# Layer A's first output rows prepared by GpSimd alone, and layer B's weight loads issued ahead of its residual rows

## The chip, the cores and the metric

The kernel runs on one core of one Trainium2 chip. The time is that of one execution in device microseconds (us). Three runs of the kernel before gave 2417.16, 2417.48 and 2418.24 us; their median is 2417.48. In this text the engines have the names that the profile gives them: PE is TensorE (matrix products), DVE is VectorE, ACT is ScalarE, POOL is GpSimd, and SP is SyncE, which here only issues transfers. Each engine works through its own list of instructions in order and waits on semaphores for the others.

## The reference

Two layers of a decoder trunk over one sequence of 2048 tokens of width 1024, in float32. Layer A is causal attention with 16 heads of 64 and a forget bias; layer B is attention in a window of 128 keys with 4 key heads. What matters here is how each layer ends, with a gate, an output product and the residual:

```python
# layer A
o = fox_attention(q, k, v, log_f).reshape(b, s, WIDTH_A)
h = h + (o * jax.nn.silu(gate)) @ w_out_a[i]
# layer B
o = swa_sink_attention(q, k_shared, v_shared, sinks[j]).reshape(b, s, WIDTH_B)
h = h + (o * jax.nn.silu(gate)) @ w_out_b[j]
```

## The kernel before

A float32 product is made of three faster ones: each operand is split into a rounded high part and the low remainder (h and l in the names), and high by high, high by low and low by high are summed in PSUM. So one product of 128x128 by 128x512 over all 1024 input columns is 24 matmuls.

The program runs five stages one after the other: projections of layer A (until 592 us), attention of layer A (592 to 1434), the output product of layer A (1445 to 1622), projections of layer B (1622 to 2047), and attention of layer B with its output product (2047 to 2417).

**Attention of layer A** goes head by head. A head's 2048 queries are four chunks of 512, and a chunk `ch` needs 2·ch+2 steps of two key blocks, so there are 20 steps a head and 320 in all, numbered n from 0. Head 15, the last, has n = 300 to 319, and its last chunk n = 312 to 319. A step makes scores on PE (L1021, L1022 and masks), their exponential on ACT (L1028, L1037), a rounded copy on ACT (L1040), the low part on POOL (L1041, `pl = pf - ph`), a running sum on DVE (L1050), and three steps later (`V_LAG`) the product with the values on PE (L1065). Between the steps PE is fed matmuls of the gate (L1111), whose weights come by the loads of L1087 into the buffers `wr` and `st`, and whose results DVE and ACT finish (L1123 to L1125). The last two gate groups of 24 matmuls are kept back until the attention is through: one goes to the bank `mx`, the next to the bank `pb`. Behind them the output product begins.

**The rows of the output product** are made in pairs of heads, 128 rows by a chunk of 512 queries. For a pair, four inputs are loaded by SP: two halves of the attention's result (`om`, L1236, and `oc`, L1237), the gate (`gt`, L1238) and the reciprocals of the softmax sums (`rd`, two loads, L1241). `gated` then does five operations on 128x512: the sum of the halves (L1255), times the reciprocals (L1258), times the gate (L1261), the rounded copy on ACT (L1262), the low remainder (L1263). The product of one pair is 24 matmuls (L1303), and there are 32 pairs. The first two pairs are prepared while the attention still runs: pair 0 at step 309, pair 1 at step 316, with their loads issued at 299 and 311, all of their arithmetic on DVE but for the copy. From pair 2 on, the sum is POOL's. The loads of pairs 0, 1 and 2 use the same buffers `qn`, `wh`, `wl`, so a load waits until the pair before it has done with its buffer. The weights of the output product are split by ACT (L142) and DVE (L143) in the same stretch.

SP issues everything in the order in which the program's scheduler has put it: attention results and gate rows to be stored, the inputs of the pairs, and the kept gate groups' weights. A transfer that has to wait for a semaphore holds all those behind it.

**Attention of layer B** has steps of about 5.06 us: scores (L1386), transposes (L362), values (L1471), and twelve matmuls of the output product (L1532) between them. Two groups of 24 make a tile of 128 tokens. Each group gathers in the one bank `pb`; DVE adds the residual rows `xr` (L1538, buffer `sq`) and SP stores the sum (L1539). The rows `xr` are loaded by L1527, the weights of the product by eight loads of 1 MB (L1510, `wo`), which are issued at steps 4 to 8.

## Time and profile before

| | |
|---|---|
| median of three runs | 2417.48 us |
| profiled execution | 2418.75 us |
| its span, first to last instruction | 2417.0 us |
| PE busy in the span | 2402.1 us (99%) |
| DVE, ACT, POOL busy | 1746.5, 1261.1, 986.7 us |
| granted PE clock, mean | 0.998 |

The profiled execution is 1.27 us above the median, and 1.75 us of it lie outside the span. In rows of the timeline the first number is the start in us from the span's start, the second the duration in us, and the bracket at the end is how long the engine sat idle before it and for whom. In rows of a table by stretches the five numbers behind the first are the busy times of PE, PE's weight loads, DVE, ACT and POOL, then come the granted PE clock (1.00 is full speed), the share of the transfer engines that was busy, and GB/s. The instructions of SP are marked SPq.

### The profile page before, as it was taken

The page shows a single profiled execution, that of the slowest core. Times are in us where ns is not written, and L with a number is a line of the kernel's source. Part 1 is how long each engine was busy: PE and PEld are TensorE (multiplying, and loading weights), DVE is VectorE, ACT ScalarE, POOL GpSimd, SP SyncE. Part 2 cuts the span into 40 slices and gives each one's busy share as a digit, 9 for nine tenths or more (in the row PEclk, how much of TensorE's full clock was granted, in tenths as well). Part 3 has the DMA queues.
Part 4 walks back from the last instruction along what each step waited for, and adds up shares of the span by engine and source line. Part 5 has one row for each costly group of instructions (what it writes and reads, how often), then busy time and mean ns, then how long its engine had stood idle before and what let it go on. Part 6 is the DMA issues. An engine that isn't in the chain of part 4 may idle for free. (4 is left out here: it accounts for less than half of the span.)

```text
span 2417.0 us, 36270 instructions
## 1 busy us (share of the span) xinstructions
PE 2402.1 (99%) x11960; PEld 2028.6 (84%) x11960; DVE 1746.5 (72%) x4094; ACT 1261.1 (52%) x2504; POOL 986.7 (41%) x634
## 2 busy tenths in 40 slices
PE   9999999999999999999999999999999999999999
PEld 7888899988888888888888878888888888888887
DVE  7656667735998998988898976457766643677776
ACT  5433324322878788777878751135423321466664
POOL 0000000011887777777877752210011000388885
PEclk9999999999999999999999999999999999999999
DMA  6656555677654745575466459975434474765552
GB/s 192 203 168 190 154 152 171 194 229 231 192 153 136 223 128 171 149 232 153 124 206 156 145 165 298 300 260 153 131 97 128 149 264 143 241 214 181 183 183 75
DMA packets 357004, 436.03 MB, mean 180 GB/s; under 512 B 65296, under 2 KB 248624, under 8 KB 350640
## 3 DMA queue, kind: packets, MB, share of 16 engines
q1 hardware_dynamic: 348464, 403.30, 55.3%
q10 hardware_dynamic: 8352, 30.41, 4.4%
q8 instruction: 95, 1.56, 0.3%
q14 instruction: 93, 0.76, 0.1%
HBM read 273.69 MB, written 159.79 MB: 179 GB/s over the span
## 5 line engine op out<-in xcount | busy, mean ns | idle before, releaser
L798 PE MATMUL b<-wh,big 128*128 128x512 f32 (+3 forms) x2560 | 772.2, 374 | 1.4 <-ACT wh L509 1.3
L1041 POOL TENSOR_TENSOR big<-st,big 128x1024 fp32r<-128x1024 f32 (+1 forms) x320 | 659.1, 2080 | 248.5 <-ACT big L1040 170.5
L798 PEld LDWEIGHTS b<-wh,big 128*128 128x128 f32 x2560 | 470.6, 188 | 72.8 <-ACT wh L509 3.2
L798 PE MATMUL b<-wl,big 128*128 128x512 f32 (+3 forms) x1280 | 473.7, 370 | 0.8 <-DVE wl L510 0.8
L1050 DVE TENSOR_TENSOR ac<-ac,st 128x512 f32<-128x512 f32 (+3 forms) x576 | 353.1, 613 | 28.2 <-ACT ac L1044 13.1
L1037 ACT ACTIVATE st<-sc 128x512 f32<-128x512 f32 (+1 forms) x512 | 275.1, 583 | 107.8 <-PE sc L1031 45.8
L1065 PE MATMUL pa<-big 128*128 128x512 f32 (+3 forms) x1280 | 319.9, 366 | 0.7 <-POOL big L1041 0.6
L1040 ACT CAST big<-st 128x1024 fp32r<-128x1024 f32 (+1 forms) x320 | 294.7, 923 | 8.0
L798 PEld LDWEIGHTS b<-wl,big 128*128 128x128 f32 x1280 | 241.2, 189 | 36.7 <-DVE wl L510 4.5
L1065 PEld LDWEIGHTS pa<-big 128*128 128x128 f32 x1280 | 229.9, 190 | 37.4 <-POOL big L1041 1.9
L1021 PE MATMUL sc<-big 128*128 128x512 f32 (+3 forms) x640 | 234.2, 370 | 5.3 <-ACT st L1037 3.5
L518 ACT ACTIVATE sq<-b,r 128x512 f32<-128x512 f32 (+2 forms) x128 | 77.8, 608 | 302.2 <-PE b L798 302.2
L989 DVE TENSOR_REDUCE mt<-mx 128x1 f32<-128x384 f32 (+1 forms) x360 | 214.2, 598 | 27.1 <-PE mx L976 25.0
L1022 PE MATMUL sc<-big 67*128 67x512 f32 (+3 forms) x640 | 229.4, 367 | 0.0
L976 PE MATMUL mx<-big 66*128 66x512 f32 (+2 forms) x600 | 225.3, 379 | 0.0
L520 DVE TENSOR_REDUCE sm<-sq 128x8 f32<-128x512 f32 (+2 forms) x128 | 74.8, 585 | 140.0 <-ACT sq L518 139.9
L1111 PE MATMUL pb<-wh,wr 128*128 128x512 f32 x488 | 172.0, 395 | 0.0
L900 POOL MEMSET rot<- 128x512 bf16 x1 | 0.5, 525 | 419.0 <-PE pb L362 419.0
L1434 POOL TENSOR_TENSOR big<-big,tri 128x1024 fp32r<-128x1024 f32 x60 | 144.4, 2406 | 60.6 <-DVE big L1431 60.6
L984 DVE CUSTOM_DVE_ANT_0 mx<-mx,rot 128x384 f32<-128x384 f32 (+2 forms) x240 | 147.6, 620 | 28.0 <-PE mx L976 25.3
L1021 PEld LDWEIGHTS sc<-big 128*128 128x128 f32 x640 | 121.7, 190 | 29.2 <-ACT st L1037 5.8
L1022 PEld LDWEIGHTS sc<-big 67*128 67x128 f32 x640 | 122.2, 191 | 18.7
(285 smaller groups left out, 4125.9 us busy)
## 6 DMA issues: line engine op xcount, KB each, us to landing
wr<-wg ACTq DMA_DIRECT2D x58, 512.0 KB
va<-st SPq DMA_DIRECT2D x32, 512.0 KB
ka<-st SPq DMA_DIRECT2D x64, 256.0 KB
ut<-big SPq DMA_DIRECT2D x16, 1024.0 KB
big<-ka SPq DMA_DIRECT2D x16, 1024.0 KB
big<-qa SPq DMA_DIRECT2D x16, 1024.0 KB
qb<-st SPq DMA_DIRECT2D x64, 256.0 KB
big<-qb SPq DMA_DIRECT2D x16, 1024.0 KB
```

Of the source, the lines that this page charges most:

```text
L798: nc.tensor.matmul(ps[:, :n], u[tb // 4][:, dt, us], W[k][dt], start=(dt == 0 and i == 0), stop=(dt == NDT - 1 and i == 2),)
L976: mm = nc.tensor.matmul(ps, qb[:66, i * P : (i + 1) * P], kb[:66, k0:k1], start=True, stop=True,)
L984: nc.vector.tensor_tensor_reduce(out=ps, in0=ps, in1=mask_m[:, 512 - w :], scale=1.0, scalar=NEG, op0=ALU.add, op1=ALU.max, accum_out=f_(o),)
L989: nc.vector.reduce_max(o, ps, axis=AX.X)
L1021: nc.tensor.matmul(o, ka[:, ks], qa[:, qs], start=not (last and n_), stop=False)
L1022: nc.tensor.matmul(o, kb[:, ks], qb[:, qs], start=False, stop=not diag)
L1037: nc.scalar.activation(pf[:, off : off + w], ps[:, :w], AF.Exp, scale=HD**-0.5)
L1040: nc.scalar.copy(ph[:, :tw], pf[:, :tw])
L1041: nc.gpsimd.tensor_tensor(pl[:, :tw], pf[:, :tw], f_(ph[:, :tw]), ALU.subtract)
L1050: nc.vector.tensor_tensor(a_, a_, pf[:, off : off + w], ALU.add)
L1065: product = nc.tensor.matmul(pv[:, q0 : q0 + w], v[:, k, :], src[:, off : off + w], start=(p == 0 and n_ == 0 and i == 0), stop=(last and ...
L1111: nc.tensor.matmul(ps, w[:, dt // 2 % 2, wk, dt % 2, :], us[dt][uk], start=(dt == 0 and i == 0), stop=(dt == NDT - 1 and i == 2),)
```

## The change

In layer A, the five operations of pair 0 are all put on POOL, one behind each of the steps 288, 290, 292, 294 and 296, with its loads issued from step 284 on. The five operations of pair 1 are also all on POOL, behind its last low part (the operation of L1041) of step 319; its loads are issued from step 300 on. The rounded copy that ACT made is now POOL's third operation, which writes the product in the rounded type. In layer B, the weight loads of a step are issued before the step's matmuls of the output product and not at its end, and the first tile's residual rows are loaded in the middle of each of its two groups and not ahead of it. The loads of the later tiles' rows stay where they were but for the order against the PSUM allocation.

```diff
--- before.py
+++ after.py
@@ -43,8 +43,8 @@
 SUM_LAG = 5
 LOAD_AT = 7
 
-PREP_LOAD_AT = (299, 311)
-PREP_AT = (309, 316)
+PREP_LOAD_AT = (284, 300)
+PREP_AT = (288, 290, 292, 294, 296)
 
 RAW_AT = 302
 
@@ -119,11 +119,17 @@
         self.t.gated_load(s // NDT, s % NDT, self.tiles[s])
         self.loaded = s + 1
 
-    def prepare(self, s, engine=None, pin=False, first=None):
+    def prepare(self, s, engine=None, pin=False):
         if s % 4 == 0:
             self.Y[s // 4] = self.t.sb("big", [P, 4, 2, CH], F32R)
-        self.t.gated(self.y(s), self.tiles.pop(s), engine or self.t.nc.vector, pin, first)
+        self.t.gated(self.y(s), self.tiles.pop(s), engine or self.t.nc.vector, pin)
         self.ready = s + 1
+
+    def prepare_parts(self, s):
+        if s % 4 == 0:
+            self.Y[s // 4] = self.t.sb("big", [P, 4, 2, CH], F32R)
+        self.ready = s + 1
+        return self.t.gated_parts(self.y(s), self.tiles.pop(s))
 
     def y(self, s):
         return self.Y[s // 4][:, s % 4]
@@ -1210,10 +1216,14 @@
                 raw = self.sb("big", [P, NDT // 2, D])
                 for p in range(NDT // 2):
                     op.weight_load(p, raw[:, p])
-            if n in PREP_AT:
-                op.prepare(PREP_AT.index(n), nc.vector, True, nc.vector)
             if n in PREP_LOAD_AT:
                 op.load(PREP_LOAD_AT.index(n), ("qn", "wh", "qn", "wl"))
+            if n in PREP_AT:
+                if n == PREP_AT[0]:
+                    parts = op.prepare_parts(0)
+                next(parts)
+        for _ in op.prepare_parts(1):
+            pass
         op.load(2, ("qn", "wh", "qn", "wl"))
         for item, more in zip(pending, HELD):
             feed(fed + more)
@@ -1243,7 +1253,16 @@
                 in_=d["rd"][h : h + 1, cols].to_broadcast([HD, CH]),
             )
 
-    def gated(self, y, tiles, engine, pin=False, first=None):
+    def gated_parts(self, y, tiles):
+        m, c, g, rb = tiles
+        yh, yl = (y[:, k] for k in range(2))
+        for out, a, b, op in (
+            (m, m, c, ALU.add), (m, m, rb, ALU.mult), (yh, m, g, ALU.mult),
+            (m, m, g, ALU.mult), (yl, m, f_(yh), ALU.subtract),
+        ):
+            yield self.tc.keep_in_program_order(self.nc.gpsimd.tensor_tensor(out, a, b, op))
+
+    def gated(self, y, tiles, engine, pin=False):
 
 
 
@@ -1252,9 +1271,7 @@
         nc = self.nc
         m, c, g, rb = tiles
         yh, yl = (y[:, k] for k in range(2))
-        add = (first or nc.gpsimd).tensor_tensor(m, m, c, ALU.add)
-        if pin and first is not None:
-            self.tc.keep_in_program_order(add)
+        nc.gpsimd.tensor_tensor(m, m, c, ALU.add)
         mult = engine.tensor_tensor(m, m, rb, ALU.mult)
         if pin:
             self.tc.keep_in_program_order(mult)
@@ -1523,11 +1540,11 @@
                 rows = slice(i * P, (i + 1) * P)
                 for nh in range(2) if i else (1, 0):
                     ns = slice(nh * CH, (nh + 1) * CH)
-                    xr = self.sb("sq", [P, CH])
-                    nc.sync.dma_start(out=xr, in_=res[rows, ns])
-
                     ps = self.ps("fl" if (i, nh) == (NTB - 1, 0) else "pb", [P, CH])
                     for p in range(NDT):
+                        if p == (0 if i else NDT // 2):
+                            xr = self.sb("sq", [P, CH])
+                            nc.sync.dma_start(out=xr, in_=res[rows, ns])
                         for n_, (y, k) in enumerate(((0, 0), (0, 1), (1, 0))):
                             nc.tensor.matmul(
                                 ps, yt(i, y, slice(p, p + 1))[:, 0, :],
@@ -1557,6 +1574,8 @@
                 php = self.sb("big", [P, 2, 2, 2, G, P], F32R)
             if n == V_LAG_B + NKV:
                 odd += [[self.sb(t, [P, 4, P], F32R) for _ in range(2)] for t in ("wh", "wl")]
+            for j in B_WEIGHTS_AT.get(n, ()):
+                weight_load(j)
             o = (n - O_LAG_B) * per
             feed(o + FEED_1)
             if n % NKV == 1 and NKV < n < N:
@@ -1575,8 +1594,6 @@
                     load(i + 1)
                 if g == NKV - 1 and i + 1 < NTB:
                     load_v(i + 1)
-            for j in B_WEIGHTS_AT.get(n, ()):
-                weight_load(j)
             yield
         feed(total)
```

The lines of the kernel move by 6 at the start and by 17 at the end: L1041 becomes L1047, L1087 L1093, L1236 to L1238 and L1241 become L1246 to L1248 and L1251, L1255 becomes L1274, L1532 L1549, L1527 L1547, L1510 L1527; the new function's operations are L1263.

The order in which the engines get their instructions changes in three places that matter below.

At the end of layer A's attention, on POOL. `big<-st,big` are the low parts of the last chunk's steps, `qn<-qn,wh` and its like the operations on a pair (x29 are the sums of the pairs from 3 on). Before:

```order
L1041 TENSOR_TENSOR big<-st,big 128x1024 x6
L1255 TENSOR_TENSOR qn<-qn,wh 128x512
L1041 TENSOR_TENSOR big<-st,big 128x896
L1041 TENSOR_TENSOR big<-st,big 128x384
L1255 TENSOR_TENSOR wh<-wh,wl 128x512 x29
```

and now:

```order
L1047 TENSOR_TENSOR big<-st,big 128x1024 x6
L1047 TENSOR_TENSOR big<-st,big 128x896
L1047 TENSOR_TENSOR big<-st,big 128x384
L1263 TENSOR_TENSOR qn<-qn,wh 128x512
L1263 TENSOR_TENSOR qn<-qn,wl 128x512
L1263 TENSOR_TENSOR big<-qn 128x512
L1263 TENSOR_TENSOR qn<-qn 128x512
L1263 TENSOR_TENSOR big<-qn,big 128x512
L1274 TENSOR_TENSOR qn<-qn,wh 128x512
```

Pair 1's five operations stand behind the last low part, and the sum of pair 2 (L1255, now L1274) behind them. DVE loses the eight operations of pairs 0 and 1, ACT two copies.

In the same place, on SP. `st<-wg` and `wr<-wg` are the weights of the two gate groups kept back, `wh<-oc`, `wl<-rd`, `qn<-om` and `qn<-gt` the inputs of pair 2. Before:

```order
L1237 DMA wh<-oc 128x512
L1241 DMA wl<-rd 64x512
L1236 DMA qn<-om 128x512
L1241 DMA wl<-rd 64x512
L1238 DMA qn<-gt 128x512
L1087 DMA st<-wg 128x1024
L1087 DMA wr<-wg 128x1024
L1087 DMA st<-wg 128x1024
L1236 DMA wh<-om 128x512
L1087 DMA wr<-wg 128x1024
```

and now:

```order
L1093 DMA wr<-wg 128x1024
L1093 DMA st<-wg 128x1024
L1247 DMA wh<-oc 128x512
L1251 DMA wl<-rd 64x512
L1246 DMA qn<-om 128x512
L1248 DMA qn<-gt 128x512
L1251 DMA wl<-rd 64x512
L1083 DMA om<-sq 64x512
L1132 DMA gt<-sq 128x512
L1084 DMA oc<-sq 64x512
L1093 DMA st<-wg 128x1024
L1093 DMA wr<-wg 128x1024
```

The first two weight loads serve the group in `mx`, the last two the group in `pb`. The inputs of pair 2 stood ahead of all four and waited for DVE's operations on pair 1; now they stand between the two groups' loads and wait for POOL's. `qn<-om` waits for pair 1's fourth operation and `qn<-gt` for its fifth.

In layer B, on PE, around the first tile's second group. `b` are scores, `fl` transposes, `pa` values, `pb` the output product. Before, from the end of the first group on:

```order
L1386 MATMUL b_21178<-big 128x256 x8
L362 MATMUL fl<-ident,st 128x128 x4
L1532 MATMUL pb<-big 128x512 x6
L1471 MATMUL pa<-big,qn 128x512 x2
L1471 MATMUL pa<-big,wh 128x512 x2
L1532 MATMUL pb<-big 128x512 x6
L1386 MATMUL b_21239<-big 128x256 x8
L362 MATMUL fl<-ident,st 128x128 x4
L1532 MATMUL pb<-big 128x512 x6
L1471 MATMUL pa<-big,qn 128x512 x2
L1471 MATMUL pa<-big,wh 128x512 x2
L1532 MATMUL pb<-big 128x512 x6
```

and now:

```order
L1403 MATMUL b_21178<-big 128x256 x8
L368 MATMUL fl<-ident,st 128x128 x4
L1488 MATMUL pa<-big,qn 128x512 x2
L1488 MATMUL pa<-big,wh 128x512 x2
L1403 MATMUL b_21237<-big 128x256 x8
L368 MATMUL fl<-ident,st 128x128 x4
L1488 MATMUL pa<-big,qn 128x512 x2
L1488 MATMUL pa<-big,wh 128x512 x2
L1403 MATMUL b_21296<-big 128x256
L368 MATMUL fl<-ident,st 128x128 x4
L1549 MATMUL pb<-big 128x512 x24
L1403 MATMUL b_21296<-big 128x256 x7
```

The second group's 24 matmuls were spread over two steps in four sixes; now they are one block that comes two steps later. On SP the four last weight loads stood behind the first residual rows and now stand ahead of them. On DVE the sum of the first group moves behind a whole further step.

## The prediction, made before the changed kernel was run

> **What bounds the kernel now.** The stages were read first: the table of stretches, then PE's waits.

> ```profile
> 592.00:1434.00 842.00, 835.97 (x4090) 693.57 (x4089) 750.34 (x1613) 669.49 (x1060) 660.32 (x321) 1.00 0.58 167
> 2047.00:2417.00 370.00, 366.16 (x1977) 315.22 (x1975) 266.41 (x626) 202.07 (x728) 247.91 (x168) 1.00 0.57 181
> 2400.00:2417.00 17.00, 13.16 (x59) 10.55 (x57) 3.82 (x8) 0.96 (x2) 0.00 (x0) 0.97 0.17 63
> PE sc L1021 <- ACT st L1037: 3.5, 2, 2.6
> PE sc L1021 <- ACT st L1028: 1.7, 1, 1.7
> ```

> PE is the bound in both stages that the change touches. Attention A leaves PE 6.0 us idle; two waits for the exponentials make 5.2 of them. Layer B's 3.84 us of idle time all lie in its last 17 us, behind the last product. So B has nothing to give where the change works; A can give those waits and what follows from them. The timeline shows where they lie:

> ```profile
> 1405.38 0.50 PE L1021 MATMUL sc<-big 128*128 128x512 f32 x1 [1.68 <-ACT st L1028]
> 1411.41 0.50 PE L1021 MATMUL sc<-big 128*128 128x512 f32 x1 [0.87 <-ACT st L1037]
> 1423.52 0.58 PE L1021 MATMUL sc<-big 128*128 128x256 f32 x1 [2.64 <-ACT st L1037]
> 1433.73 0.45 PE L1065 MATMUL pa<-big 128*128 128x256 f32 x2 [0.18 <-POOL big L1041]
> 1434.02 0.45 PE L1111 MATMUL mx<-wh,st 128*128 128x512 f32 x1
> 1439.82 0.50 PE L1111 MATMUL pb<-wh,st 128*128 128x512 f32 x1
> ...
> 1404.31 0.62 ACT L1262 CAST big<-qn 128x512 fp32r<-128x512 f32 x1 [4.54 <-DVE qn L1261]
> 1422.35 0.62 ACT L1262 CAST big<-qn 128x512 fp32r<-128x512 f32 x1 [4.56 <-DVE qn L1261]
> ```

> Twice ACT stands 4.5 us before a pair's rounded copy, because DVE is late with the product by the gate; the exponentials are queued behind that copy, and PE waits for them. DVE is late because POOL works beside it:

> ```profile
> 1399.45 2.29 DVE L1258 TENSOR_TENSOR qn<-qn,wl 128x512 f32<-128x512 f32 x1
> 1418.83 2.76 DVE L1258 TENSOR_TENSOR qn<-qn,wl 128x512 f32<-128x512 f32 x1
> 1421.62 0.69 DVE L1261 TENSOR_TENSOR qn<-qn 128x512 f32<-128x512 f32 x1
> 1413.40 7.64 POOL L1041 TENSOR_TENSOR big<-st,big 128x1024 fp32r<-128x1024 f32 x3 [0.51 <-ACT big L1040]
> ```

> An operation of this kind takes 0.69 us where POOL is idle (1421.62) and 2.3 to 2.8 beside POOL's low parts. The last PE wait has a second price, the granted clock (the number behind the five busy times):

> ```profile
> 1423.00:1424.00 1.00, 0.48 (x2) 0.49 (x3) 1.00 (x2) 1.00 (x3) 0.00 (x0) 0.50 0.54 164
> 1428.00:1429.00 1.00, 1.00 (x4) 0.72 (x3) 1.00 (x1) 1.00 (x2) 1.00 (x2) 0.50 0.31 107
> 1429.00:1430.00 1.00, 1.00 (x5) 0.82 (x4) 1.00 (x2) 1.00 (x2) 1.00 (x1) 0.67 1.20 188
> ```

> From 1423.5 until about 1429.3 PE ran at half rate, and 5.8 us of such work lose 2.9. Behind the gaps of 1.68 and 0.87 the clock stayed at 1.00.

> **The change, part by part: what layer A gains.** With the ten operations of pairs 0 and 1 off DVE and ACT, the copies that held the exponentials are gone. Gain: 1.68 + 0.87 + 2.64 + 0.18 + 2.9 = 8.3 us. PE would then come to the `mx` group at 1434.0 - 8.3 = 1425.7, and POOL's last low part, for which the last values product waited 0.18 us, ends at about T = 1425.4.

> **What pair 0 costs.** POOL gets five operations in steps 288 to 296. One takes 1.30 us, by the sum that POOL makes for pair 2:

> ```profile
> 1427.36 1.30 POOL L1255 TENSOR_TENSOR qn<-qn,wh 128x512 f32<-128x512 f32 x1
> 1362.00:1374.00 12.00, 12.00 (x60) 9.91 (x59) 10.88 (x24) 8.75 (x15) 10.18 (x5) 1.00 0.06 14
> ```

> In the 12 us at the end of head 14, POOL is busy 10.18, so 1.8 are free per 12, and a step has 2.4. An operation of 1.30 every two steps (4.8 us, 0.7 free) makes POOL late by about 0.6 each, 3 us over the five. Values are used three steps behind, which covers most of it: I take 0.5 us, between 0 (cover holds) and 3 (none does).

> **What pair 1 costs.** Its five operations begin at T and take 5 x 1.30 = 6.5 us, so the remainder is done at 1431.9 if nothing disturbs it. DVE's weight splits (L143) run in the same stretch, and these two engines disturb each other:

> ```profile
> 1427.88 6.88 DVE L143 TENSOR_TENSOR big<-big 128x1024 fp32r<-128x1024 f32 x3 [0.38 <-PE pb L1111]
> 1428.60 5.08 POOL L1041 TENSOR_TENSOR big<-st,big 128x896 fp32r<-128x896 f32 x2
> 1375.51 3.10 POOL L1041 TENSOR_TENSOR big<-st,big 128x896 fp32r<-128x896 f32 x2 [1.90 <-PE sc L1027]
> 1435.29 1.21 DVE L143 TENSOR_TENSOR big<-big 128x1024 fp32r<-128x1024 f32 x1
> ```

> The same two low parts took 5.08 us beside three splits and 3.10 elsewhere. So POOL loses between 0 and 2.0; I take 1.0, since some splits will run before T: done at 1432.9. Nobody needs pair 1 itself before the output product. But SP's loads of pair 2 wait for it, and the weights of the `pb` group stand behind them, as the order shows. SP's issue times:

> ```profile
> 1421.62 0.47 SPq L1241 DMA_DIRECT2D wl<-rd  x1
> 1423.71 0.33 SPq L1238 DMA_DIRECT2D qn<-gt  x1
> 1424.14 0.38 SPq L1087 DMA_DIRECT2D st<-wg  x1
> 1434.83 0.47 SPq L1077 DMA_DIRECT2D om<-sq  x1
> 1435.35 0.59 SPq L1078 DMA_DIRECT2D oc<-sq  x1
> 1440.59 0.33 SPq L1237 DMA_DIRECT2D wl<-oc  x1
> 1444.24 1.29 POOL L1255 TENSOR_TENSOR wh<-wh,wl 128x512 f32<-128x512 f32 x1 [10.56 <-DMA wl<-oc]
> ```

> Behind the remainder come `qn<-gt`, `wl<-rd`, `om<-sq`, `gt<-sq` (priced like `qn<-gt`) and `oc<-sq`: 0.33 + 0.47 + 0.47 + 0.33 + 0.59 = 2.2 us. `st<-wg` is issued at 1435.1. How long 512 KB take is not shown; 256 KB took 3.65 from issue to use (1440.59 to 1444.24). The bounds are 3.65 and twice that; I take 4.5, near the lower, because the issue and the landing signal are paid once. It lands at 1439.6. PE wants it when the `mx` group and the softmax sums are through, 1439.82 - 1434.02 = 5.8 us behind 1425.7, at 1431.5. A new PE wait of 8.1 us. Its bounds: 1431.9 + 2.2 + 3.65 - 1431.5 = 6.2, and 1433.9 + 2.2 + 7.3 - 1431.5 = 11.9. The lower does not depend on T, which moves both sides.

> Such a gap is longer than the 2.64 that halved the clock, so I add 2.9, between 0 and 2.9. [...]

> [...]

> Behind the group, pair 2's inputs have landed by then and its arithmetic has the gate group's 5.4 us and two pairs' products ahead of it. Pair 3 on keeps its distance from the group. No cost. Layer A: -8.3 + 0.5 + 8.1 + 2.9 = +3.2 us, with bounds -8.3 + 6.2 = -2.1 and -8.3 + 3 + 11.9 + 2.9 = +9.5.

> **What layer B costs.** The first residual rows were issued at 2101.10, ahead of the last four weight loads; now they follow them:

> ```profile
> 2105.09 2.65 SPq L1510 DMA_DIRECT2D big<-wo  x3
> 2115.00:2118.00 3.00, 3.00 (x17) 2.55 (x16) 2.75 (x8) 2.00 (x9) 2.49 (x2) 1.00 1.02 416
> 2118.00:2121.00 3.00, 3.00 (x19) 2.62 (x18) 2.69 (x7) 1.62 (x7) 2.17 (x3) 1.00 0.83 227
> ```

> Issued at 2107.7, they join a queue that keeps the transfer engines full until about 2117.5, where the rate falls; there they land. DVE's sum (0.69) frees the one bank `pb` at 2118.2 at the earliest. Meanwhile PE, without matmuls of the product to fill in, reaches the block of 24 sooner:

> ```profile
> 2112.37 1.12 PE L1386 MATMUL b<-big 128*128 128x256 f32 x8
> 2113.33 0.60 PE L362 MATMUL fl<-ident,st 128*128 128x128 f32 x4
> 2113.68 1.64 PE L1532 MATMUL pb<-big 128*128 128x512 f32 x6
> 2115.51 2.40 POOL L1434 TENSOR_TENSOR big<-big,tri 128x1024 fp32r<-128x1024 f32 x1 [1.25 <-DVE big L1431]
> ```

> A bare step is 0.96 of scores, 0.35 of transposes and 0.92 of values, 2.2 us; two of them, one more score and its transposes end at 2112.4 + 4.9 = 2117.3. The second step's values need POOL's masking of the first step's weights (2115.51 + 2.40 = 2117.9), and DVE's sum stands behind this step's own work: some 1.2 us more for half the values and the transposes, 0.7 for the sum, gives 2119.9. PE loses 2.6 us, in pieces under 1.7, so the clock stays. Bounds: 0 if all of it is late by chance elsewhere, and 5 if the rows land at 2121. A gain is excluded, since PE has no idle time there. The weights themselves came in time before (no wait of PE), so that they are issued earlier is worth nothing.

> Sum: +3.2 + 2.6 = +5.8 us, on 2418.75 a time of 2424.5, and on the median, 1.27 below, 2423.3.

> **The rivals.** First, no new wait: `st<-wg` comes in time because PE gets to it later or SP sooner than I think. Then A keeps its 8.3 less 0.5, B costs 0 to 2.6: 2409.7 to 2412.3. For it speaks that every DVE and ACT cause is really gone; against it, that even the lower bound leaves 6.2 us. Chance 0.14.

> Second, even: the new wait is at its lower bound and the clock comes back at once, as it did behind 1.68: -8.3 + 0.5 + 6.2, with B at 0 to 2.6, is -1.6 to +1.0, or 2415.9 to 2418.5. Against it speaks the half rate at 1423.5. Chance 0.22.

> Third, slower than the forecast, by one mechanism: POOL's last operations and DVE's splits hold each other, so that the remainder is done 2 us or more later and the transfer shares its engines with pair 2's loads. It decides from a landing at 1443.4 on: a wait of 11.9 and +7.0 in A; with B at 0 to 5, 2424.5 to 2429.5, slower than before by more than the forecast. Chance 0.12.

> That POOL's earlier work has no place in steps 288 to 296 would be part of the forecast, at most 2.5 us more.

> **How the numbers follow.** The forecast, 2423.3 with its own range of 2418.5 to 2427, has 0.52. What this kernel's measurement can tell from no change is 0.2%, 4.8 us: 2412.6 and 2422.3 are the limits. Of the forecast 0.33 lies above the upper limit, 0.19 below. Slower: 0.33 + 0.12 = 0.45. Same: 0.19 + 0.22 = 0.41. Faster: 0.14. The range takes half of the first rival and most of the third: 2411 to 2429.

> **What would show it.** In the changed profile, no wait of PE for L1034 or L1043 between 1400 and 1425, and no ACT copy of a pair; POOL's five L1263 in a row from about 1425 to 1432 or 1433; SP's `st<-wg` behind `oc<-sq` at about 1435 and a PE wait of 6 to 12 us on the first matmul of `pb` on line L1117, with the clock at 0.50 behind it. In B, a block of 24 L1549 that starts 2 to 3 us later than the work ahead of it allows, waiting for DVE's L1555, which waits for `sq<-h`. The forecast is wrong if the `pb` group follows the `mx` group without a gap, or if PE still waits for exponentials of head 15.

## The result and the profile after

The changed kernel took 2430.31 us (median of four runs, 2429.12 to 2432.11), the kernel before 2417.38 on the same chip. The ratio is 1.0052 with a 95% interval of 1.0039 to 1.0066: slower by 12.9 us, where +5.8 had been forecast. The way and the two places were right, and both were priced too low. The profiled execution took 2429.12 us, the fastest of the four, with a span of 2427.4, which is 10.4 us more than the span before; the execution traced before, 2418.75 us, was 1.4 above the median of 2417.38. What the other executions add has no trace. Of all runs below, one execution ran at a granted clock of 0.654 and took 3369.14 us; it is left out of every comparison.

PE's waits after the change, the four rows that bear on it (waited for, us in total, times, longest), and then the like of the last one before:

```profile
PE pb L1117 <- DMA st<-wg: 11.1, 1, 11.1
PE pb L1549 <- DVE sq L1555: 1.7, 1, 1.7
PE pa L1488 <- DMA big<-wo: 0.8, 1, 0.8
PE pa L1071 <- POOL big L1047: 0.6, 2, 0.4
...
PE pa L1065 <- POOL big L1041: 0.6, 2, 0.4
```

The waits for the exponentials, 5.2 us before, are gone. Three new ones have come: one of 11.1 us for the weights of the last kept gate group, one for DVE's sum in layer B, and a smaller one at layer B's values, which the profile puts down to a load of weights. The last row reads 0.6 as before, so the operations that POOL got in steps 288 to 296 cost PE nothing.

**Layer A.** PE's timeline after the change, at the first matmul of the `mx` group, of the `pb` group and of the output product:

```profile
1424.67 0.44 PE L1117 MATMUL mx<-wh,st 128*128 128x512 f32 x1
...
1441.67 0.76 PE L1117 MATMUL pb<-wh,st 128*128 128x512 f32 x1 [11.10 <-DMA st<-wg]
...
1449.89 5.38 PE L1320 MATMUL b<-big 128*128 128x512 f32 x23
```

Before, these were at 1434.02, 1439.82 and 1445.40, the last by PE's timeline before:

```profile
1445.40 8.32 PE L1303 MATMUL b<-big 128*128 128x512 f32 x36
```

So PE was 9.35 us ahead, then 1.85 behind, then 4.49 behind. The last step is the clock: the group of 24 took 8.22 us from its start to the product's, 5.58 before. The table by stretches shows the clock at half (behind the five busy times) from 3.1 us into the gap until 5.7 us after PE had begun again:

```profile
1433.72:1447.37 13.65, 5.70 (x14) 4.48 (x15) 1.81 (x4) 0.63 (x1) 1.67 (x2) 0.50 0.79 243
```

SP's timeline after the change shows the queue, and POOL's what it waits for:

```profile
1432.88 0.32 SPq L1248 DMA_DIRECT2D qn<-gt  x1
1433.25 0.48 SPq L1251 DMA_DIRECT2D wl<-rd  x1
1433.82 0.55 SPq L1083 DMA_DIRECT2D om<-sq  x1
1434.46 0.54 SPq L1132 DMA_DIRECT2D gt<-sq  x1
1435.05 0.46 SPq L1084 DMA_DIRECT2D oc<-sq  x1
1435.56 0.76 SPq L1093 DMA_DIRECT2D st<-wg  x1
...
1424.30 2.27 POOL L1263 TENSOR_TENSOR qn<-qn,wh 128x512 f32<-128x512 f32 x1
1426.65 2.16 POOL L1263 TENSOR_TENSOR qn<-qn,wl 128x512 f32<-128x512 f32 x1
1428.89 1.29 POOL L1263 TENSOR_TENSOR big<-qn 128x512 fp32r<-128x512 f32 x1
...
1431.59 1.26 POOL L1263 TENSOR_TENSOR big<-qn,big 128x512 fp32r<-128x512 f32 x1
...
1421.73 5.92 DVE L149 TENSOR_TENSOR big<-big 128x1024 fp32r<-128x1024 f32 x3
```

POOL's fifth operation ends at 1432.85, and 0.03 us later SP issues `qn<-gt`; four more issues follow, then the weights, 5.0 us later than PE could have used them (1430.57, where its wait begins). They land 6.1 us after their issue (1435.56 to 1441.67). POOL's first two operations ran beside DVE's splits and took about 0.9 us longer each than the last three.

**Layer B.** Of the changed kernel, SP's issue of the first residual rows and DVE's sum, and then PE's steps around the block of 24; the last line is from PE's timeline before:

```profile
2112.61 0.69 SPq L1547 DMA_DIRECT2D sq<-h  x1
...
2125.09 0.69 DVE L1555 TENSOR_TENSOR sq<-pb,sq 128x512 f32<-128x512 f32 x1 [1.58 <-DMA sq<-h]
...
2116.82 1.12 PE L1403 MATMUL b<-big 128*128 128x256 f32 x8
...
2125.83 7.35 PE L1549 MATMUL pb<-big 128*128 128x512 f32 x24 [1.70 <-DVE sq L1555]
2133.02 1.00 PE L1403 MATMUL b<-big 128*128 128x256 f32 x7
...
2137.49 1.12 PE L1403 MATMUL b<-big 128*128 128x256 f32 x8
...
2127.59 1.12 PE L1386 MATMUL b<-big 128*128 128x256 f32 x8
```

The scores at 2116.82 stood at 2112.37 before, 4.45 us earlier; those at 2137.49 have their like at 2127.59 before, 9.90 earlier. So layer B loses 5.45 us. The rows took 12.5 us from issue to use. The block took 7.19 us to the next start where 24 matmuls take 5.44 (four sixes of 1.36, from 2116.09 to 2117.45 before), because here too the clock fell:

```profile
2123.21:2126.62 3.41, 1.56 (x8) 1.09 (x8) 1.83 (x4) 1.75 (x4) 3.22 (x3) 1.00 0.94 192
2126.62:2130.04 3.42, 3.42 (x9) 2.67 (x8) 2.47 (x7) 1.88 (x9) 3.17 (x3) 0.50 0.88 227
```

No single gap here is over 1.7 us, but PE was busy only 1.56 of the 3.41 us ahead of the fall. Of the 5.45 us, 2.7 are the waits that the profile names (0.21, 0.78 and 1.70), 1.75 the block's slower clock, and the rest lies in smaller pieces.

### The profile page after: what moved, and what is told of

Its sections match the earlier page's. It is cut to its first block, busy times and chain, and to the rows that moved or that the text cites. A ratio compares the mean times of both kernels' runs of the same rounds, so it can differ in the third digit from the quotient of the medians.

```text
span 2427.4 us, 36286 instructions
## 1 busy us (share of the span) xinstructions
PE 2404.1 (99%) x11960; PEld 2030.3 (84%) x11960; DVE 1730.5 (71%) x4086; ACT 1259.8 (52%) x2502; POOL 999.6 (41%) x644
## 3 DMA queue, kind: packets, MB, share of 16 engines
q8 instruction: 95, 1.56, 0.3%
## 4 chain that ended last, share of the span: by engine, by line
PE 95%; DMA 2%; DVE 1%; POOL 1%; ACT 0%; issue 0%; SPq 0%; POOLq 0%; ACTq 0%
PE b L804 31%; PE pa L1071 10%; PE pb L1117 7%; PE pb L1549 7%; PE sc L1027 5%; PE b L1320 5%; PE sc L1028 5%; PE mx L982 5%; PE b L766 4%; PE b L1403 2%; PE pb L766 2%; PE pa L1488 2%; PE fl L368 1%; PE pa L368 1%; PE pb L368 1%; PE pa L766 1%
## 5 line engine op out<-in xcount | busy, mean ns | idle before, releaser
L1047 POOL TENSOR_TENSOR big<-st,big 128x1024 fp32r<-128x1024 f32 (+1 forms) x320 | 657.7, 2076 | 236.9 <-ACT big L1046 162.7
L1043 ACT ACTIVATE st<-sc 128x512 f32<-128x512 f32 (+1 forms) x512 | 274.6, 582 | 109.7 <-PE sc L1037 46.5
L1027 PE MATMUL sc<-big 128*128 128x512 f32 (+3 forms) x640 | 233.7, 369 | 0.1
L1028 PE MATMUL sc<-big 67*128 67x512 f32 (+3 forms) x640 | 229.2, 367 | 0.0
L1117 PE MATMUL pb<-wh,wr 128*128 128x512 f32 x488 | 171.6, 395 | 0.0
L1027 PEld LDWEIGHTS sc<-big 128*128 128x128 f32 x640 | 121.5, 190 | 23.0 <-ACT st L1043 1.5
L539 POOL TENSOR_TENSOR ro<-qn,rot 128x64 f32<-128x64 f32 (+1 forms) x48 | 15.6, 325 | 297.6 <-DVE qn L530 292.0
```

What stands on the lines that cost most here:

```text
L1027: nc.tensor.matmul(o, ka[:, ks], qa[:, qs], start=not (last and n_), stop=False)
L1028: nc.tensor.matmul(o, kb[:, ks], qb[:, qs], start=False, stop=not diag)
L1043: nc.scalar.activation(pf[:, off : off + w], ps[:, :w], AF.Exp, scale=HD**-0.5)
L1047: nc.gpsimd.tensor_tensor(pl[:, :tw], pf[:, :tw], f_(ph[:, :tw]), ALU.subtract)
L1117: nc.tensor.matmul(ps, w[:, dt // 2 % 2, wk, dt % 2, :], us[dt][uk], start=(dt == 0 and i == 0), stop=(dt == NDT - 1 and i == 2),)
```

## The experiments

Times of the kernel before are those beside the runs: 2418.51 for the first four, 2418.53 for the next three, 2418.69 for the two after them, 2417.63 for the last. The ratio is to these.

**Layer A's part alone, and layer B's part alone.** Each is the change without the other's edits.

> Layer A's part of the change alone; layer B as before. Theory (the kept gate group's weights stand on SP behind pair 2's loads, which wait for POOL; the PE wait and the half rate behind it cost more than the 9.3 us gained): the PE wait of 11 us stays, the output product of layer A starts 4.5 us later than before, and the time is 2420 to 2423. Rival (most of the loss is layer B's and layer A breaks even): 2416 to 2419.

> Layer B's part alone; layer A as before. Theory (the first tile's residual rows land behind 3 to 4 MB of weights, PE's next group waits, and the clock falls to half): +5.5 to +8 us, 2423 to 2425.5, with a block of 24 matmuls that takes 7 us or more and waits 1 to 2 us for DVE's sum. Rival (the loss in layer B comes only because layer A's part shifts the transfers there): 2417 to 2419.

Layer A alone: 2423.61 us, ratio 1.0021 (1.0011 to 1.0030), +5.1. Layer B alone: 2425.78, ratio 1.0029 (1.0018 to 1.0039), +7.3. The sum, 12.4, is about the whole loss of 12.9, so the two add up and both rivals fall. Both times are a little above what was expected, 2420 to 2423 and 2423 to 2425.5. Layer B's waits, from the timelines of its run:

```profile
2108.76 0.62 SPq L1530 DMA_DIRECT2D sq<-h  x1
...
2121.93 0.69 DVE L1538 TENSOR_TENSOR sq<-pb,sq 128x512 f32<-128x512 f32 x1 [3.40 <-DMA sq<-h]
...
2122.68 7.66 PE L1532 MATMUL pb<-big 128*128 128x512 f32 x24 [3.52 <-DVE sq L1538]
```

The rows come 13.2 us after their issue here, and PE waits 3.5 us, not the 1 to 2 that were expected.

**Pair 2's loads behind the gate groups' weights,** in the changed kernel, and in layer A's part alone:

```diff
-        op.load(2, ("qn", "wh", "qn", "wl"))
         for item, more in zip(pending, HELD):
             feed(fed + more)
             values(item, pin=more > 0)
...
         for _ in filler:
             pass
+        op.load(2, ("qn", "wh", "qn", "wl"))
```

> The changed kernel with pair 2's loads issued behind the kept gate groups' weights. Theory (the order on SP makes the wait): the PE wait on these weights is gone or under 1 us, the group's clock stays at 1.00, layer A gains some 9 us on before, layer B still loses 5.5 to 8: 2413 to 2417. Rival (the weights are late because the transfer engines are full, or POOL holds DVE and so the group): a wait of 5 us or more stays, over 2420.

> Layer A's part alone with pair 2's loads issued behind the kept gate groups' weights; layer B as before. Theory: nothing of the new waits is left, 2407 to 2410. Rival (pair 2 or a later pair is now late and the output product waits for it): 2413 to 2418, with a PE wait on L1320.

The first took 2418.59 us (median of its other nine executions), ratio 1.0000 (0.9990 to 1.0010), the second 2411.04 us, ratio 0.9970 (0.9958 to 0.9982), 7.5 us faster than the kernel before. Both medians are some us above what was expected (2413 to 2417, 2407 to 2410), but the order does what the theory says. The first lies between the theory's range and its rival's; it is what the second gains and layer B's part loses, -7.5 and +7.3. PE's timeline of the second, at the same three places as above:

```profile
1425.01 0.50 PE L1117 MATMUL mx<-wh,st 128*128 128x512 f32 x1
...
1430.89 0.50 PE L1117 MATMUL pb<-wh,st 128*128 128x512 f32 x1
...
1436.47 8.32 PE L1320 MATMUL b<-big 128*128 128x512 f32 x36
```

There is no wait between the groups, and the product starts 8.9 us before its time in the kernel before (1445.40). POOL's work, DVE's splits and the number of transfers are the same as in layer A's part alone; only SP's order differs. So the loss of layer A comes from that order alone. The first of the two has no profile to read.

**Two more POOL operations on pair 1,** in layer A's part alone:

```diff
-            (m, m, c, ALU.add), (m, m, rb, ALU.mult), (yh, m, g, ALU.mult),
+            (m, m, c, ALU.add), (m, m, rb, ALU.mult), *((yh, m, g, ALU.mult),) * (1 + more),
```

> Layer A's part alone, with POOL doing pair 1's third operation (the rounded product by the gate) three times over instead of once; it writes the same values. Theory (SP's queue waits for pair 1's fifth operation): two more operations of 1.3 us make the PE wait before the last kept gate group 2.6 us longer, about 14 us, and the time 2.6 us longer than layer A's part alone, about 2426. Rival (the wait is set by the transfer engines or by DVE): the wait stays at 11 to 11.5 us and the time at 2423.6.

2425.93 us, ratio 1.0031 (1.0018 to 1.0045), 2.3 us above layer A's part alone. PE's wait in layer A's part alone, then in this run:

```profile
PE pb L1117 <- DMA st<-wg: 11.4, 1, 11.4
```

```profile
PE pb L1117 <- DMA st<-wg: 12.9, 1, 12.9
```

SP's issue of the weights in the two, in the same order:

```profile
1435.88 0.58 SPq L1093 DMA_DIRECT2D st<-wg  x1
```

```profile
1438.57 0.58 SPq L1093 DMA_DIRECT2D st<-wg  x1
```

The issue moved by 2.7 us, as the theory says. The wait grew by 1.5 only, because PE came 0.6 us later to the group and the weights landed 5.8 us after their issue instead of 6.3. The wait does follow POOL, so the rival falls; the size of the landing is not constant. Nor is the clock's price. The stretch in which the full clock came back, in the two, in the same order:

```profile
1447.00:1449.00 2.00, 2.00 (x8) 1.56 (x7) 0.00 (x0) 0.00 (x0) 1.24 (x1) 0.76 0.76 193
```

```profile
1446.00:1448.00 2.00, 2.00 (x8) 1.58 (x7) 0.00 (x0) 0.00 (x0) 0.00 (x0) 0.67 0.73 218
```

A mean clock of 0.76 and of 0.67 over 2 us puts its return at 1447.96 and at 1447.3. The group began at 1442.23 in layer A's part alone and at 1444.39 in this run, so half rate lasted 5.7 us of work behind the shorter gap and 2.9 behind the longer.

**Pair 1 as the later pairs, behind the attention,** in layer A's part alone:

```diff
-        for _ in op.prepare_parts(1):
-            pass
+        op.prepare(1, nc.vector)
```

> Layer A's part alone, with pair 1 prepared behind the attention as the later pairs are (sum on POOL, products and remainder on DVE, rounded copy on ACT); the order puts the kept gate groups' weights ahead of pair 2's loads again. Theory: the wait of 11 us is gone, as it comes from the order on SP and not from the work; 2409 to 2413, the upper end if the output product waits for pair 1, which is ready later. Rival (the work on pair 1 itself must stand before the gate group): over 2418.

2418.59 us, ratio 1.0001 (0.9992 to 1.0011): the rival's number, over 2418, but not its mechanism. The wait before the `pb` group is gone, as the theory says. PE lost the time earlier: it came to the `mx` group at 1435.88, 10.9 us later than in layer A's part alone (1424.99). The scheduler had put a pair's sum on POOL and the pairs' transfers into the attention, and there POOL stood idle with the low parts behind it. From the timelines of POOL, ACT and PE in this run:

```profile
1389.54 1.26 POOL L1273 TENSOR_TENSOR qn<-qn,wh 128x512 f32<-128x512 f32 x1 [5.20 <-DVE sq L1131]
...
1390.38 0.58 ACT L1081 COPY sq<-pa 128x512 f32<-128x512 f32 x1 [2.51 <-DMA oc<-sq]
...
1391.02 0.50 PE L1071 MATMUL pa<-big 128*128 128x512 f32 x1 [2.48 <-ACT sq L1081]
```

This wait of PE, its longest there, was not for POOL but for ACT's copy of a result, and that for a store; for POOL's low parts PE waited 2.4 us in all. That the store was held up by the pairs' transfers is argued and not shown.

**The rows on ACT's queue,** in layer B's part alone:

```diff
-                            nc.sync.dma_start(out=xr, in_=res[rows, ns])
+                            (nc.sync if i else nc.scalar).dma_start(out=xr, in_=res[rows, ns])
```

> Layer B's part alone, with the first tile's two residual row loads issued by ACT instead of SP, so that they stand in another queue than the weights. Theory (the rows are late because they stand behind the weights in SP's queue): they land within 7 us of their issue, PE does not wait for DVE's sum, 2416.5 to 2420. Rival (the transfer engines are full, whatever the queue): they land 10 us or more after their issue, and PE waits 2 us or more at the second group: over 2421.

2420.76 us, ratio 1.0011 (1.0001 to 1.0020). This was to compare the queues and did not: the first rows were now issued at 2100.04, ahead of the weights. The second rows' issue stood in ACT's own list until 2111.57, and ACT's cast behind it made DVE and then PE late. From the timelines of ACT and PE in this run (DVE had stood 3.23 us before its own operation behind that cast):

```profile
2111.57 0.33 ACTq L1530 DMA_DIRECT2D sq<-h  x1
...
2115.71 1.66 PE L1532 MATMUL pb<-big 128*128 128x512 f32 x6 [1.62 <-DVE sq L1538]
```

**What stands ahead of the rows,** in layer B's part alone. One run issues the last two weight loads at step 10, so that the rows stand behind 2 MB instead of 4; one loads the first rows ahead of the weights, which keep their new place at the start of the step:

```diff
-B_WEIGHTS_AT = {4: (0,), 5: (1,), 6: (2,), 7: (3,), 8: (4, 5, 6, 7)}
+B_WEIGHTS_AT = {4: (0,), 5: (1,), 6: (2,), 7: (3,), 8: (4, 5), 10: (6, 7)}
```

```diff
+            if n == O_LAG_B:
+                first.append(self.sb("sq", [P, CH]))
+                nc.sync.dma_start(out=first[0], in_=res[:P, CH:])
             for j in B_WEIGHTS_AT.get(n, ()):
                 weight_load(j)
...
+                        if i == 0 and nh == 1:
+                            xr = first[0]
```

> Layer B's part alone, with the last two of its eight weight loads issued at step 10 instead of step 8, so that 2 MB and not 4 stand ahead of the first residual rows. Theory (the rows wait for the bytes ahead of them in SP's queue, at some 0.42 MB per us): they land about 5 us sooner than the 13 us after issue of layer B's part alone, that is 8 us after it, PE waits for DVE's sum under 1 us, and the time is 2418 to 2421. Rival (the late sum has another cause, such as DVE's or POOL's order): the wait of 2 us or more stays, over 2422.

> Layer B's part alone, but the first tile's first residual rows are loaded at step 8 ahead of the weights; the weights keep their place at the start of the step. Theory: the whole loss of layer B comes from these rows; without it 2417 to 2419.5, no different from the kernel before, since the earlier weights are worth nothing. Rival (the weights' earlier place itself costs or gains by moving other transfers): more than 2 us either way.

With the rows ahead: 2418.20 us, ratio 0.9998 (0.9989 to 1.0008). So the earlier weights cost and gain nothing that can be told, and the whole loss of layer B comes with the place of these rows. But the place brings PE's order with it. PE's timeline of this run, in the step in which the changed kernel has no matmul of the product:

```profile
2115.44 1.64 PE L1534 MATMUL pb<-big 128*128 128x512 f32 x6
...
2117.85 1.56 PE L1534 MATMUL pb<-big 128*128 128x512 f32 x6
```

These are the sixes of the kernel before; the block of 24 is gone, here and in the three other runs that move the rows. So the price of late rows and that of the block are not told apart by this run. With 2 MB ahead: 2422.88, ratio 1.0014 (1.0004 to 1.0024), the rival's number and not the theory's. The timelines of SP and PE, and the semaphore group of DVE's sum, where its wait for the rows stands (ns, least, median and most, and the first start):

```profile
2105.57 0.65 SPq L1530 DMA_DIRECT2D sq<-h  x1
...
2117.86 2.93 PE L1532 MATMUL pb<-big 128*128 128x512 f32 x6 [4.10 <-DVE sq L1538]
```

```profile
L1538 DVEq EVENT_SEMAPHORE  x33: 21/50/7621, 2109.4 to 2414.6; - x33
```

The rows came at 2109.4 + 7.6 = 2117.0, 11.4 us after their issue and not 8. So the sum did wait for the rows, which the rival denies, and late rows cost PE 4.10 us without a block of 24 too; the price was wrong. That brought up another reading, that a transfer issued into full engines lands only when all the backlog is through, with what is issued behind it. It was tested by putting the rows between the second and the third of the last four weight loads, with 2 MB ahead as before, and 2 MB behind instead of 1:

```diff
             for j in B_WEIGHTS_AT.get(n, ()):
+                if j == 6:
+                    first.append(self.sb("sq", [P, CH]))
+                    nc.sync.dma_start(out=first[0], in_=res[:P, CH:])
                 weight_load(j)
```

> Layer B's part alone, with the first residual rows issued between the fourth and the fifth MB of the weights that count here: 2 MB of the last four stand ahead of them as in the run with two loads at step 10, but 2 MB and not 1 stand behind them. Theory, as it now stands (a transfer that is issued into full engines lands only when the whole backlog is through, what is issued behind it included): the rows land about 2.5 us later after their issue than the 11.5 us of that run, about 14, PE waits 5 us or more for DVE's sum, 2423 to 2427. Rival (transfers of one queue land in the order of issue, and 11.5 us is what stands ahead): about 11.5 us again, a PE wait of some 4 us, and the same time as that run, 2421 to 2423.

2421.93 us, ratio 1.0018 (1.0008 to 1.0027), within the rival's range. The same views of this run, and two stretches with its clock:

```profile
2105.80 0.58 SPq L1566 DMA_DIRECT2D sq<-h  x1
...
2115.27 1.66 PE L1534 MATMUL pb<-big 128*128 128x512 f32 x6 [2.45 <-DVE sq L1540]
```

```profile
L1540 DVEq EVENT_SEMAPHORE  x33: 21/50/5970, 2108.5 to 2409.4; - x33
```

```profile
2114.00:2116.00 2.00, 0.73 (x3) 0.65 (x4) 1.41 (x3) 0.00 (x0) 0.00 (x0) 1.00 1.01 413
2116.00:2118.00 2.00, 2.00 (x10) 1.63 (x10) 2.00 (x6) 0.24 (x1) 0.54 (x1) 1.00 1.04 400
```

The rows came at 2114.5, 8.7 us after their issue, while the engines stayed full until 2118. So the new reading falls, and the numbers fit the first one in its sign: fewer bytes ahead, an earlier landing (12.5 and 13.2 us with 4 MB, 11.4 and 8.7 with 2). Each number is of one execution, and PE's order differs between the pairs. It does not stand as a price: the same 2 MB gave 8.7 in one execution, the second fastest of its ten, and 11.4 in another, the slowest of its ten. From 2106 to 2110 this run moved 255 and then 387 GB/s (two stretches of 2 us), the one with two loads at step 10 151 and 267; why is open.

## Why the prediction was wrong

The waits that it named came in both layers, its sizes were too small, in layer B it put the clock at nothing, and the measured time lies 1.3 us above its range. By its own steps:

- **What layer A gains:** forecast 8.3, measured 9.35. The copies and their waits went as described; the gain was taken a little low, 0.2 of it because the half rate before lasted until 1429.66 and not 1429.3.
- **Pair 0 in steps 288 to 296:** forecast 0.5, not seen. That the use three steps later covered it all fits this.
- **POOL's five operations:** forecast done at 1432.9, measured 1432.85. POOL lost 1.8 us beside DVE (2.27 and 2.16 us for the first two operations, where one takes 1.30), inside the bounds of 0 to 2.0; it began 1.1 us sooner. DVE's three splits had begun at 1421.73, 2.6 us before pair 1, and ended at 1427.65, in POOL's second operation.
- **The wait before the `pb` group:** forecast 8.1 (6.2 to 11.9), measured 11.1. This is the first term that was mis-sized: the landing of `st<-wg`, put at 4.5 us and measured at 6.1. Of the rest, 0.9 is that PE got there sooner and 0.5 that the five issues took 2.7 us and not 2.2. I had taken the landing near its lower bound because "the issue and the landing signal are paid once"; but five transfers had been issued in the 2.7 us ahead of it. That these slowed it is argued. Of the reason the traces show the issue alone (0.33 us for 256 KB and 0.38 for 512, `qn<-gt` and `st<-wg` in the kernel before); no run shows the signal.
- **The clock behind it:** forecast 2.9, measured 2.64 (8.22 against 5.58). The clock came back after 5.7 us of work here (1441.67 to 1447.37) and after 6.1 in the kernel before (1423.52 to 1429.66).
- **Layer A in all:** forecast +3.2; its own part of the profile says +4.5, and alone it measured +5.1.
- **Layer B:** forecast +2.6 with an upper bound of 5; the profile says 5.45, and alone it measured +7.3. This is the step that failed. Two things in it were wrong. The rows were to land at 2117.5, 9.8 us after their issue; they took 12.5 and 13.2. I read the end of the queue from a row in which GB/s fell from 416 to 227, while the share of busy engines was still 0.83 there, and 1.03 until 2119: the engines were not through. And "in pieces under 1.7, so the clock stays" was a wrong rule drawn from two isolated gaps. The pieces came close together (PE busy 1.56 of 3.41 us), and the clock fell: 7.19 us for a block of 5.44. In this execution the clock is what was missing: the named waits, 2.7 us, were close to the 2.6 forecast for all of layer B. In the run of layer B alone the longest gap was 3.52, with a block of 7.5 (2122.68 to the next start).

The rival that came closest was the third, slower than the forecast, at 2424.5 to 2429.5, and not by its mechanism: it wanted POOL done 2 us later, which did not happen, and a landing from 1443.4 on, where it was 1441.67. The chance of 0.45 for slower was the largest of the three, and slower is what came. The rest between the profile's 10.4 us and the medians' 12.9 lies in which executions were traced: 1.2 under the median after, 1.4 above it before. That the clock's part varies between executions was seen: in the run with two more POOL operations it came back 2.9 us after a longer gap, in layer A's part alone 5.7 us after a shorter one. One of the eight executions of layer B's part alone had a mean clock of 1.000 and took 2420.60 us, the others 2424.73 to 2427.24. That the clock makes the spread of the medians fits this and is not shown.

## What to carry to other kernels

Before work is moved to an engine that is free, look at what the transfers that wait for it hold up behind them in the issuing queue: here five POOL operations cost 11.1 us of PE, not because PE needed them but because a load that it did need stood behind one that waited for them. Putting the urgent weights ahead of that load turned +5.1 us into -7.5. A load whose data is needed soon does not go behind megabytes whose data is needed later, and how long it then takes is not to be read from a rate: behind 4 MB the rows took 12.5 and 13.2 us here, behind 2 MB 8.7 and 11.4, so allow the whole backlog, to be safe. Several short waits close together can cost the clock as a long one does: in layer B none was over 1.7 us here, and the clock stood at half for 3.41 us behind them.

## What the runs showed of the hardware

**How busy PE had been ahead of it.** In stretches of 3.41 us, counted from the falls, PE had been busy 1.46 and 0.46 us ahead of the two falls in the kernel before, and 0.26, 1.56 and 0.00 ahead of the three in the changed kernel, the last at 2427.00. From 20 us on, the least busy stretch at the full clock with no fall behind it had 1.74 (from 1402.35) in the first and 2.42 (from 2119.80) in the second. At half rate, the clock stayed there behind stretches with 2.73 us (the kernel before), 0.00, 0.00 and 2.29 (the changed one), and came back behind three with 3.41. These are two executions, and what decides it they do not show. A gap of 2.64 us stands both in the kernel before and in the run with the rows between (its longest wait for the exponentials reads 2.6, and the two rows leave 1.07 and 1.57 us idle):

```profile
1419.42:1422.83 3.41, 1.46 (x8) 0.77 (x6) 3.38 (x3) 0.48 (x1) 1.62 (x1) 1.00 0.32 79
1422.83:1426.25 3.42, 2.73 (x9) 2.45 (x10) 2.93 (x6) 3.42 (x7) 1.24 (x1) 0.50 0.66 218
```

```profile
1417.79:1421.21 3.42, 2.35 (x12) 1.39 (x10) 3.35 (x3) 0.00 (x0) 2.51 (x1) 1.00 0.46 138
1421.21:1424.62 3.41, 1.84 (x11) 1.62 (x12) 3.02 (x6) 3.01 (x6) 0.34 (x1) 1.00 0.57 162
```

In the first, 1.95 us of the gap lay in one stretch, and the clock was at half for the next two; in the second, the clock stayed. So a gap of one and the same length cost nothing more in one execution and a second price in another. Half rate lasted 2.9 us of work behind the gap in the run with two more POOL operations, 5.7 in the changed kernel and 6.1 in the kernel before, which makes such a gap worth 1.5 to 3.1 us on top of itself, as an estimate.
